# Tree attention: K and Q of heads 16 to 47 and 56 to 63 laid side by side by GpSimd before they are transposed

## The chip, the cores and the metric

The kernel runs on one core of one Trainium2 chip. The core has five engines with a queue of their own each: TensorE (PE, with its weight loads listed apart as PEld), VectorE (DVE), ScalarE (ACT), GpSimd (POOL) and SyncE (SP), and 16 DMA engines that they share. Each queue runs in order; queues wait for one another by semaphores. The metric is device time in microseconds (us) from launch to end, as the median of several executions.

## The reference

There are 96 heads (8 x 12) of 512 rows of 64 numbers in fp32. Row i is a node of a binary tree, and may look at itself and at its ancestors alone:

```python
mask = np.zeros((seq, seq))
for i in range(seq):
    mask[i, i] = 1
    parent = i
    while parent > 0:
        parent = (parent - 1) // 2
        mask[i, parent] = 1

scores = np.einsum('bhqd,bhkd->bhqk', Q, K) * scale
scores = scores + (1 - mask) * (-1e9)
weights = np.exp(scores - np.max(scores, axis=-1, keepdims=True))
weights = weights / (np.sum(weights, axis=-1, keepdims=True) + 1e-10)
return np.einsum('bhqk,bhkd->bhqd', weights, V).astype(np.float32)
```

## The kernel before

**Tiling.** Heads go in pairs: iteration i works on two heads, which stand in the upper and the lower 64 partitions of the scores' operands, and there are 48 pairs (NP). Pairs 0 to 7 (heads 0 to 15) have a layout of their own ("narrow"); from pair 8 on ("wide", WIDE = 8) K and Q come in with two heads side by side over the partitions. K and Q are loaded in blocks of 8 heads (KB), fp32 in HBM to bf16 in SBUF, into the tiles kst and qst, each with four buffers. V is loaded in blocks of 16 heads (VB = 16) into vst (three buffers), and its rows are then spread by DVE, ACT and POOL into the tiles vt (two sets), in the order that the tree needs (`spread`, L364).

**One iteration** has these steps, each named by a letter in the strings that set the order of PE's work (FIRST for i below 9, then "SVK" for odd i and "SVQ" for even i):

- S: the scores of pair i. Matmuls with mask codes (L511, L544) and with K and Q (L519, L554) go into PSUM, ACT takes the exponential (L529, L560).
- V: the values of pair i - 1. 20 small matmuls (L605) into ob; DVE takes the reciprocal of the sums (L651) and multiplies (L653) into the output tile of.
- K or Q: a turn. `wide_k` or `wide_q` transposes K or Q of two later pairs (four heads) through PE into ktp or qtp in PSUM, and DVE copies these into kq (L470, L474, L478 for K, L493 for Q). K of pairs 4b and 4b + 2 (block b) is turned in iterations 4b - 3 and 4b - 1, Q in 4b - 2 and 4b.
- DVE's and ACT's share of V's spreading.

**A turn** has eight slots. In blocks that are not in LAID each slot takes two transposes of 64 columns, one for each head, straight from kst or qst (`turn_slot`, L450). In blocks of LAID, which are 8 to 11 (heads 64 to 95), POOL has first laid the rows of two heads next to each other (`lay`, L433), in the one tile besideK or the one tile besideQ, with a half (g) for each turn; the turn then takes one transpose of 128 columns for a slot (L441). Since there is one such tile for each name, a half can be laid anew only when PE has turned what stood in it.

**The order on POOL** is a list written out by hand (`pool_program`): the loads, the stores, its share of the spreading, and the lays. An entry is put into the program at the first iteration in which `ready` allows it, and POOL runs them in that order. Each DMA issued by POOL takes the next of eight semaphores (DMASW0 to DMASW7) and waits until the DMA that had it eight places earlier has landed.

**The order within V**: the products are `firsts` (128 columns of e), `wholes` (128) and `halves` (64). Up to pair 27 `halves` come last, from pair 28 (4 * LAID[0] - 4) they stand between the other two.

Of the kernel before, what the change touches and what calls it, by code (L numbers as in the profile page):

```python
# [119 lines left out]
def kernel(  # L120
# [7 lines left out]
    nc = tc.nc  # L128
# [7 lines left out]
    WIDE = 8  # L136
    KB, VB, VO = 8, 16, 16
    EIGHT = 2
    LAID = (8, 9, 10, 11)
    assert NH % VB == 0  # L140

    fp32 = mybir.dt.float32
# [90 lines left out]
    issued = {(name, h) for name in ("kst", "qst") for h in (0, 1)}  # L233
# [35 lines left out]
    def head(i, a):  # L269

        return 2 * i + a if i < WIDE else 4 * (i // 2) + i % 2 + 2 * a
# [151 lines left out]
    def slots(st, i):  # L423
        return st[2 * i // KB].rearrange("p (g x) t d -> p g (x t) d", x=2)

    def lay(name, b):

        st = {"kst": ksts, "qst": qsts}[name][b]
        assert all((name, h) in issued for h in range(KB * b, KB * b + KB))
        laid[name, b] = two = beside[name[0].upper()]  # L430
        for g in range(KB // 4):
            src = st[:, 4 * g:4 * g + 4, :, :].rearrange("p (a x) t d -> p (x t) a d", x=2)
            nc.gpsimd.tensor_copy(  # L433
                out=two[:, g, :, :, :].bitcast(int32), in_=src.bitcast(int32)
            )

    def turn_slot(dst, name, i, s, out):

        two = laid.get((name, 2 * i // KB))
        if two is not None:  # L440
# [5 lines left out]
            return  # L446
        assert 2 * i // KB not in LAID
        st = slots({"kst": ksts, "qst": qsts}[name], i)
# [143 lines left out]
    def values(i):  # L592

        if i < NP - 1:
            obs[i] = ob = psO.tile([P, 2, 512], fp32, name="ob")
        else:
            obs[i] = ob = psS.tile([P, 2, 512], fp32, name="s1")
        e1, e2, vt = ets[i], e2s[i % NE], vts[(head(i, 0) // VB) % NV]

        vtile = VTILE if i < WIDE else WVTILE  # L600
        parts = EIGHT_PARTS if head(i, 0) >= VB * EIGHT else PARTS[i >= WIDE]
        assert all(("vt", n, head(i, a)) in issued for n in parts for a in range(2))

        def product(e, a, t, tile_v, lo=0, hi=128, **flags):
            nc.tensor.matmul(  # L605
                out=ob[lo:hi, a, 65 * t:65 * t + 65],
                lhsT=e[:, a, PLACE[t], lo:hi],
                rhs=vt[vtile[tile_v][0]][:, head(i, a) % VB, vtile[tile_v][1], 0:D + 1],
                **flags,
            )  # L610

        def firsts(a):
            for t in range(4):
                product(e1, a, t, 0, start=t == 0, stop=False)

        def halves(a, last=True):
            for t in (0, 1):
                product(e2, a, t, 1 + SELF[t], 0, 64, start=False, stop=last and t == 1)
                product(e2, a, t, 1 + t, 64, 128, start=False, stop=last and t == 1)

        def wholes(a, last=False):
            for t in (2, 3):
                product(e2, a, t, 1 + t, start=False, stop=last and t == 3)

        if i == NP - 1:
            for a in range(2):
                firsts(a)
                wholes(a)
                halves(a)
        elif i >= 4 * LAID[0] - 4:  # L630
            for a in range(2):
                firsts(a)
            for a in range(2):
                halves(a, False)
            for a in range(2):
                wholes(a, True)
        else:
            for a in range(2):
                firsts(a)
                wholes(a)  # L640
            for a in range(2):
                halves(a)
# [33 lines left out]
    def pool_program():  # L676

        ops = [
            (load_k, 2, 2), (load_q, 2, 2), (load_v, 0, 4), (load_v, 4, 4),
            (load_k, 4, 4), (load_q, 4, 4), (load_k, 8, 4),  # L680
            (load_q, 8, 4), (load_v, 8, 8), (load_k, 12, 4),
            (load_q, 12, 4), (load_k, 16, 8), (load_q, 16, 4), (load_rows, 1, "upper"),
            (load_rows, 1, "even"), (load_rows, 1, "odd"), (load_q, 20, 4),
            (load_k, 24, 8), (load_q, 24, 8), (load_rows, 2, "upper"),
            (load_k, 32, 8), (load_leaves, 2, 0), (load_leaves, 2, 1),
            (load_q, 32, 8), (load_rows, 3, "upper"),
            (spread_pool, (1, "Z0", 8, 16), (1, "Z1", 8, 16)),
            (load_k, 40, 8), (load_q, 40, 8), (load_leaves, 3, 0), (load_leaves, 3, 1),
            (spread_top, 2, 0, 16), (spread_pool, (2, "Z0", 0, 16), (2, "Z1", 0, 16)),
            (load_q, 48, 8), (spread_pool, (2, "X", 0, 16)),  # L690
            (load_k, 48, 8), (spread_pool, (2, "N", 0, 16)),
            (load_rows, 4, "upper"), (spread_top, 3, 0, 16),
            (load_k, 56, 8), (load_q, 56, 8), (load_leaves, 4, 0), (load_leaves, 4, 1),
            (spread_pool, (3, "X", 0, 16), (3, "N", 0, 16), (3, "Z0", 0, 16), (3, "Z1", 0, 16)),
            (load_k, 64, 8), (store_rows, 0, 2), (load_q, 64, 8), (store_rows, 2, 4),
            (load_k, 72, 8), (spread_top, 4), (store, nc.gpsimd, 4, 12), (lay, "kst", 8),
            (load_q, 72, 8), (spread_pool, (4, "X", 0, 16), (4, "N", 0, 16)),
            (lay, "qst", 8), (load_rows, 5, "upper"),
            (spread_pool, (4, "Z0", 0, 16), (4, "Z1", 0, 16)),
            (load_leaves, 5, 0), (load_leaves, 5, 1), (load_k, 80, 8), (load_q, 80, 8),  # L700
            (store, nc.gpsimd, 16, 8), (lay, "kst", 9), (load_k, 88, 8), (load_q, 88, 8),
            (lay, "qst", 9), (store, nc.gpsimd, 24, 8), (store, nc.gpsimd, 32, 16),
            (spread_top, 5), (lay, "kst", 10), (store, nc.gpsimd, 48, 16), (lay, "qst", 10),
            (spread_pool, (5, "X", 0, 16), (5, "N", 0, 16)),
            (spread_pool, (5, "Z0", 0, 16), (5, "Z1", 0, 16)),
            (lay, "kst", 11), (store, nc.gpsimd, 64, 8), (lay, "qst", 11),
            (store, nc.gpsimd, 72, 8), (spread_leaves, 5, 1),
            (store, nc.gpsimd, 80, 8), (store, nc.gpsimd, 88, 4),
        ]
        return ops  # L710
# [54 lines left out]
    def spread_by(copy, table, i):  # L765

        for args in table.get(i, []):
            spread(copy, *args)

    program = pool_program()  # L770

    def pool(i):
# [23 lines left out]
    for i in range(NP + 1):  # L796
        steps = FIRST[i] if i < len(FIRST) else "SVK" if i % 2 else "SVQ"
        for step in steps:
            if step == "S" and i < NP:
                scores1(i)  # L800
                scores2(i)
            if step == "V" and i >= 1:
                values(i - 1)
                norm(i - 1)
                valued = True
            if step == "K" and kdone < NP:
                kdone = turn("kst", kdone)
            if step == "Q" and qdone < NP:
                qdone = turn("qst", qdone)
            if step == "W":  # L810
                nc.scalar.copy(
                    out=codes[64:64 + CODE_ROWS, 1280:1536], in_=codes[0:CODE_ROWS, 1280:1536]
                )
            if step == "X":
                spin("s1" if valued else "ob", 2)
            if step == "D":
                spread_by(nc.vector.tensor_copy, BY_VECTOR, i)
            if step == "A":
                spread_by(nc.scalar.copy, BY_SCALAR, i)
        if "D" not in steps:  # L820
            spread_by(nc.vector.tensor_copy, BY_VECTOR, i)
        if "A" not in steps:
            spread_by(nc.scalar.copy, BY_SCALAR, i)
        pool(i)
# [32 lines left out]
```

## Time and profile before

| What | Value |
|---|---|
| Time, median of 3 runs | 133.55 us (133.35 to 133.63) |
| The profiled execution: its own time | 133.8 us |
| Its span, first to last instruction | 131.9 us |
| Mean granted TensorE clock | 0.978 |
| HBM read, written | 37.96 MB, 12.58 MB |
| Mean DMA rate | 245 GB/s |

The DMA rate counts bytes as they are moved into SBUF: loads turn fp32 into bf16, so that stages of pure loading show about 200 GB/s and stages of pure storing about 400. Busy time of an engine is the time covered by its instructions; issuing a DMA counts on POOL in these rows as a DMA_DIRECT2D instruction. In the timeline a row is: start, time covered, engine, line of the kernel, operation, what is written <- what is read, how many instructions are merged, and in brackets the idle time before it with what ended it. A row of stages is: the stage, its length, then busy time (and instructions) of the engines, the granted clock, the DMA share and GB/s.

### The profile page before, as it was taken

How to read it: one execution, taken by the hardware profiler on the slowest of the kernel's cores; microseconds unless marked ns; L12 is line 12 of the kernel's file. 1: busy time of each engine (PE TensorE's matmuls, PEld its weight loads, DVE VectorE, ACT ScalarE, POOL GpSimd, SP SyncE). 2: the span in 40 equal slices, each digit the busy share in tenths (PEclk: the TensorE clock that was granted, in tenths of full speed). 3: DMA queues.
4: the chain of work that ended last, by engine and by line, in shares of the span. 5: the costliest groups of instructions: out<-in, count | busy, mean ns of one | idle time of the engine just before them, and what ended most of it. 6: DMA issues, size and time to landing. Idle time of an engine off the chain costs nothing.

```text
span 131.9 us, 5281 instructions
## 1 busy us (share of the span) xinstructions
PE 114.7 (87%) x2286; PEld 80.4 (61%) x2289; DVE 108.8 (82%) x261; ACT 94.4 (72%) x153; POOL 87.1 (66%) x118
## 2 busy tenths in 40 slices
PE   6883999999789699899899999999988999999920
PEld 2351576676566476666577677677765766776610
DVE  3438569988999989989999999999999999877350
ACT  4358268989768957968858787787868668688900
POOL 6994624245623998799951899999999977802200
PEclk9999599999999999999999999999999999999996
DMA  3999999999999999999999999999999999999984
GB/s 122 216 190 196 198 199 205 199 199 207 206 200 205 204 202 208 209 202 205 202 208 204 244 236 305 338 204 207 203 288 285 228 391 406 400 402 402 397 315 148
DMA packets 29719, 32.28 MB, mean 245 GB/s; under 512 B 1488, under 2 KB 26704, under 8 KB 29696
## 3 DMA queue, kind: packets, MB, share of 16 engines
q0 software_dynamic: 28416, 30.68, 115.2%
q1 hardware_dynamic: 864, 0.93, 2.1%
q10 hardware_dynamic: 416, 0.33, 1.0%
q8 instruction: 18, 0.29, 0.8%
q14 instruction: 5, 0.04, 0.1%
HBM read 37.96 MB, written 12.58 MB: 383 GB/s over the span
## 4 chain that ended last, share of the span: by engine, by line
DVE 38%; PE 24%; DMA 14%; POOL 10%; issue 5%; ACT 3%; ACTq 1%; POOLq 0%
DVE of L653 12%; DVE vt L364 11%; DMA kst<-in_K_dram 8%; PE ob L605 8%; DMA qst<-in_Q_dram 6%; POOL vt L364 5%; DVE rec L651 3%; PE s L511 3%; DVE kq L493 3%; DVE kq L470 3%; DVE kq L478 3%; DVE kq L474 3%; PE s L519 2%; ACT e L560 2%; PE s L544 1%
## 5 line engine op out<-in xcount | busy, mean ns | idle before, releaser
L529 ACT ACTIVATE e<-s 128x1024 bf16<-128x1024 f32 x40 | 40.9, 1023 | 20.7 <-PE s L519 20.1
L605 PE MATMUL ob<-vt,e 128*128 128x65 bf16 (+1 forms) x940 | 39.8, 198 | 6.0 <-DVE of L653 3.0
L605 PEld LDWEIGHTS <-e 128*128 128x128 bf16 (+1 forms) x960 | 31.7, 103 | 15.9 <-DVE of L653 5.1
L560 ACT ACTIVATE e<-s 128x384 bf16<-128x384 f32 x80 | 34.7, 491 | 0.0
L653 DVE TENSOR_TENSOR of<-ob,rec 128x512 f32<-128x512 f32 x47 | 32.5, 691 | 1.6
L364 POOL COPY vt<-vst 32x512 int32<-32x512 int32 (+1 forms) x38 | 31.0, 816 | 2.9 <-PE ob L605 1.2
L364 DVE COPY vt<-vst 32x1024 bf16<-32x1024 bf16 (+6 forms) x54 | 26.8, 497 | 2.3 <-DMA vst<-in_V_dram 1.3
L662 POOL DMA_DIRECT2D out_dram<-of x13 | 12.1, 928 | 12.7 <-DVE of L653 9.2
L511 PE MATMUL s<-codes 40*128 40x512 bf16 x96 | 19.3, 398 | 0.7 <-ACT e L525 0.4
L519 PE MATMUL s<-kq 64*128 64x512 bf16 x96 | 18.5, 380 | 0.0
L651 DVE RECIPROCAL rec<-ob 128x8 f32<-128x8 f32 x47 | 9.6, 204 | 8.8 <-PE ob L605 8.0
L554 PEld LDWEIGHTS <-kq 64*128 64x128 bf16 x320 | 12.1, 94 | 4.8
L554 PE MATMUL s<-kq 64*128 64x160 bf16 (+1 forms) x320 | 14.6, 208 | 0.0
L544 PE MATMUL s<-codes 40*128 40x384 bf16 x80 | 13.6, 333 | 0.3
L493 DVE COPY kq<-qtp 128x1024 bf16<-128x1024 bf16 x20 | 13.6, 681 | 0.0
L256 POOL DMA_DIRECT2D qst<-in_Q_dram x11 | 8.3, 752 | 6.8 <-DMA vst<-in_V_dram 2.6
L525 ACT ACTIVATE e<-s 128x1024 bf16<-128x1024 f32 x8 | 8.2, 1022 | 6.0 <-PE s L519 5.9
L544 PEld LDWEIGHTS <-codes 40*128 40x128 bf16 x80 | 6.1, 94 | 7.9 <-issue 1.2
L256 POOL DMA_DIRECT2D kst<-in_K_dram x10 | 7.6, 760 | 3.9 <-PE ob L605 2.8
L470 DVE COPY kq<-ktp 128x256 bf16<-128x256 bf16 x20 | 8.3, 415 | 0.3 <-PE ktp L450 0.3
L474 DVE COPY kq<-ktp 128x256 bf16<-128x256 bf16 x20 | 8.3, 415 | 0.0
L478 DVE COPY kq<-ktp 128x512 bf16<-128x512 bf16 x20 | 8.3, 414 | 0.0
(49 smaller groups left out, 139.4 us busy)
## 6 DMA issues: line engine op xcount, KB each, us to landing
kst<-in_K_dram POOLq DMA_DIRECT2D x10, 512.0 KB, 13.2
out_dram<-of POOLq DMA_DIRECT2D x5, 1024.0 KB, 13.9
qst<-in_Q_dram POOLq DMA_DIRECT2D x9, 512.0 KB, 14.5
out_dram<-of POOLq DMA_DIRECT2D x2, 2048.0 KB, 20.8
vst<-in_V_dram POOLq DMA_DIRECT2D x12, 256.0 KB, 14.9
vst<-in_V_dram POOLq DMA_DIRECT2D x6, 512.0 KB, 14.3
out_dram<-of POOLq DMA_DIRECT2D x1, 1536.0 KB, 10.7
qst<-in_Q_dram POOLq DMA_DIRECT2D x5, 256.0 KB, 11.9
```

The lines of the kernel that those rows point to most:

```text
L256: return nc.gpsimd.dma_start(out=kept[b][:, h0 % KB:h0 % KB + n, :, :].rearrange("p (g x) t d -> p g (x t d)", x=2), in_=wide[:, h0 // 2:( ...
L364: return copy(out=dst, in_=src)
L493: nc.vector.tensor_copy(out=qq[:, :, 0:16, :].rearrange("p b u c -> p b (u c)"), in_=halves)
L511: nc.tensor.matmul(out=sp[:, a, :], lhsT=(k1code if i < WIDE else k1wide)[64 * a:64 * a + CODE_ROWS, :], rhs=(q1code[64 * a:64 * a + CODE_ ...
L519: nc.tensor.matmul(out=sp[:, a, :], lhsT=keys(i, a, TOP), rhs=qTs[i][64 * a:64 * a + 64, :, :].rearrange("p t c -> p (t c)"), start=False, ...
L529: ) if i < WIDE else nc.scalar.activation(
L544: nc.tensor.matmul(out=flat[:, a, :, :].rearrange("p u (t c) -> p u t c", t=4)[:, :, :, 16:64], lhsT=k2wide[64 * a:64 * a + CODE_ROWS, :], ...
L554: nc.tensor.matmul(out=flat[:, a, :, lo:hi], lhsT=keys(i, a, WTILE2[t]), rhs=qT[64 * a:64 * a + 64, :, lo:hi], start=False, stop=t == 1, s ...
L560: nc.scalar.activation(out=e2s[i % NE][:, a, :, 32:128].rearrange("p t (r u) -> p t r u", u=2), in_=flat[:, a, :, :].rearrange("p u (t r) ...
L605: nc.tensor.matmul(out=ob[lo:hi, a, 65 * t:65 * t + 65], lhsT=e[:, a, PLACE[t], lo:hi], rhs=vt[vtile[tile_v][0]][:, head(i, a) % VB, vtile ...
L651: nc.vector.reciprocal(out=rec[:, a:a + n, :, :], in_=o4[:, a:a + n, :, D:D + 1])
L653: nc.vector.tensor_tensor(out=ofs[g][:, first:last + 1:step, :, :], in0=o4[:, a:a + n, :, 0:D], in1=rec[:, a:a + n, :, :].to_broadcast([P, ...
```

## The change

Blocks 2, 3, 4, 5 and 7 (heads 16 to 47 and 56 to 63) join LAID. `lay` can lay one half alone. The point from which V takes its other order stays at pair 28, now as LATE. In POOL's list the lays of these blocks are added, the spreading of the top rows of V's block 3 (`spread_top`, 3) moves behind the loads of block 7 and the leaves of V's block 4, and the third and fourth of four small stores are issued one at a time.

```diff
-    LAID = (8, 9, 10, 11)
+    LAID = (2, 3, 4, 5, 7, 8, 9, 10, 11)
+    LATE = 28
...
-    def lay(name, b):
+    def lay(name, b, g0=0, g1=2):
...
-        for g in range(KB // 4):
+        for g in range(g0, g1):
...
-        elif i >= 4 * LAID[0] - 4:
+        elif i >= LATE:
...
-            (load_k, 24, 8), (load_q, 24, 8), (load_rows, 2, "upper"),
-            (load_k, 32, 8), (load_leaves, 2, 0), (load_leaves, 2, 1),
-            (load_q, 32, 8), (load_rows, 3, "upper"),
-            (spread_pool, (1, "Z0", 8, 16), (1, "Z1", 8, 16)),
-            (load_k, 40, 8), (load_q, 40, 8), (load_leaves, 3, 0), (load_leaves, 3, 1),
+            (load_k, 24, 8), (load_q, 24, 8), (load_rows, 2, "upper"), (lay, "kst", 2),
+            (load_k, 32, 8), (lay, "qst", 2, 0, 1), (load_leaves, 2, 0), (load_leaves, 2, 1),
+            (load_q, 32, 8), (lay, "qst", 2, 1, 2), (load_rows, 3, "upper"),
+            (spread_pool, (1, "Z0", 8, 16), (1, "Z1", 8, 16)), (lay, "kst", 3),
+            (load_k, 40, 8), (load_q, 40, 8), (lay, "qst", 3),
+            (load_leaves, 3, 0), (load_leaves, 3, 1), (lay, "kst", 4),
             (spread_top, 2, 0, 16), (spread_pool, (2, "Z0", 0, 16), (2, "Z1", 0, 16)),
-            (load_q, 48, 8), (spread_pool, (2, "X", 0, 16)),
+            (load_q, 48, 8), (lay, "qst", 4), (spread_pool, (2, "X", 0, 16)),
             (load_k, 48, 8), (spread_pool, (2, "N", 0, 16)),
-            (load_rows, 4, "upper"), (spread_top, 3, 0, 16),
-            (load_k, 56, 8), (load_q, 56, 8), (load_leaves, 4, 0), (load_leaves, 4, 1),
+            (load_rows, 4, "upper"), (lay, "kst", 5),
+            (load_k, 56, 8), (load_q, 56, 8), (lay, "qst", 5),
+            (load_leaves, 4, 0), (load_leaves, 4, 1), (spread_top, 3, 0, 16),
             (spread_pool, (3, "X", 0, 16), (3, "N", 0, 16), (3, "Z0", 0, 16), (3, "Z1", 0, 16)),
-            (load_k, 64, 8), (store_rows, 0, 2), (load_q, 64, 8), (store_rows, 2, 4),
-            (load_k, 72, 8), (spread_top, 4), (store, nc.gpsimd, 4, 12), (lay, "kst", 8),
+            (load_k, 64, 8), (store_rows, 0, 2), (load_q, 64, 8), (store_rows, 2, 3),
+            (lay, "kst", 7), (store_rows, 3, 4),
+            (load_k, 72, 8), (lay, "qst", 7), (spread_top, 4), (store, nc.gpsimd, 4, 12), (lay, "kst", 8),
```

How this stands in the queues, at three places. The line numbers of the changed kernel are one higher than before in these functions; x2 is two instructions alike.

On POOL, where block 4 (heads 32 to 39) is about to be turned; the rows start with the two loads of V's leaves of block 3. Before:

```order
L294 DMA vst<-in_V_dram 32x8x512 x2
L364 COPY vt_0_107<-vst 32x16x32 x4
L364 COPY vt_1_108<-vst 32x32x32 x2
L256 DMA qst<-in_Q_dram 128x4x512
L364 COPY vt_2_109<-vst 32x32x32
```

and now:

```order
L295 DMA vst<-in_V_dram 32x8x512 x2
L434 COPY besideK<-kst 128x512 x2
L365 COPY vt_0_107<-vst 32x16x32 x4
L365 COPY vt_1_108<-vst 32x32x32 x2
L257 DMA qst<-in_Q_dram 128x4x512
L434 COPY besideQ<-qst 128x512 x2
L365 COPY vt_2_109<-vst 32x32x32
```

K of block 4 has come in between the DMA issues and six V copies, Q of block 4 behind these and behind another load.

On PE, the first turn of Q of block 4, with the last product of V ahead of it. Before:

```order
L605 LDWEIGHTS e_1_103
L605 MATMUL ob<-vt_1_114,e_1_103 64x65
L450 LDWEIGHTS qst [waits DMASW7_49]
L450 MATMUL qtp<-ptile,qst 64x2x64
L450 LDWEIGHTS qst
```

and now:

```order
L606 LDWEIGHTS e_1_103
L606 MATMUL ob<-vt_1_114,e_1_103 64x65
L442 LDWEIGHTS besideQ [waits Pool_49]
L442 MATMUL qtp<-ptile,besideQ 128x2x64
L442 LDWEIGHTS besideQ
```

The turn waited for a load that had landed, and now waits for POOL's copy; of 16 pairs of instructions eight are left.

On POOL, the lay of K of block 8 (heads 64 to 71), with a store ahead of it and the load of Q of block 9 behind. Before:

```order
L662 DMA out_dram<-of 128x12x256 [waits DMASW3_49]
L433 COPY besideK<-kst 128x512 [waits DMAHW1_49,DMASW4_49,Pool_49]
L433 COPY besideK<-kst 128x512
L256 DMA qst<-in_Q_dram 128x4x512
L364 COPY vt_2_109<-vst 32x32x32 [waits PE_49,Pool_49]
```

and now:

```order
L663 DMA out_dram<-of 128x12x256 [waits DMASW3_49]
L434 COPY besideK<-kst 128x512 [waits DMASW4_49,PE_49,Pool_49]
L434 COPY besideK<-kst 128x512 [waits PE_49]
L257 DMA qst<-in_Q_dram 128x4x512
L365 COPY vt_2_109<-vst 32x32x32 [waits Pool_49]
```

Both halves now wait for PE, the second for the second turn of block 7, which stood in it.

More of the change, by code (lines that the diff above doesn't have):

```diff
@@ L424, in slots @@
         return st[2 * i // KB].rearrange("p (g x) t d -> p g (x t) d", x=2)
-    def lay(name, b):
+    def lay(name, b, g0=0, g1=2):
         st = {"kst": ksts, "qst": qsts}[name][b]
-        assert all((name, h) in issued for h in range(KB * b, KB * b + KB))
+        assert all((name, h) in issued for h in range(KB * b + 4 * g0, KB * b + 4 * g1))
         laid[name, b] = two = beside[name[0].upper()]
-        for g in range(KB // 4):
+        for g in range(g0, g1):
             src = st[:, 4 * g:4 * g + 4, :, :].rearrange("p (a x) t d -> p (x t) a d", x=2)
```

## The prediction

> **What bounds the kernel now.** I read the busy rows and the slices of the page first, then busy time by stage, then the timeline of the engines that wait on one another in heads 16 to 63. The page:
>
> ```profile
> span 131.9 us, 5281 instructions
> PE 114.7 (87%) x2286; PEld 80.4 (61%) x2289; DVE 108.8 (82%) x261; ACT 94.4 (72%) x153; POOL 87.1 (66%) x118
> DVE  3438569988999989989999999999999999877350
> POOL 6994624245623998799951899999999977802200
> DMA  3999999999999999999999999999999999999984
> ```
>
> Two resources are full almost throughout: the DMA engines from the second slice on, and VectorE (DVE) from a fifth of the span on. GpSimd (POOL) has gaps in the first half and none from slice 24 to 32. By stage (columns: stage, length, then busy PE, PEld, DVE, ACT, POOL, clock, DMA share, GB/s):
>
> ```profile
> 40.00:48.00 8.00, 6.63 (x154) 4.74 (x153) 7.40 (x17) 5.76 (x10) 5.76 (x9) 1.00 1.30 203
> 48.00:56.00 8.00, 7.36 (x175) 5.35 (x172) 7.78 (x19) 6.53 (x11) 6.58 (x9) 1.00 1.25 206
> 56.00:64.00 8.00, 7.56 (x179) 5.48 (x180) 7.37 (x18) 5.98 (x11) 7.82 (x10) 1.00 1.31 204
> 64.00:72.00 8.00, 7.43 (x175) 5.32 (x170) 7.71 (x19) 5.89 (x10) 4.37 (x6) 1.00 1.25 206
> 88.00:96.00 8.00, 7.84 (x150) 5.81 (x146) 7.75 (x18) 6.38 (x12) 7.91 (x11) 1.00 1.30 204
> ```
>
> Between 40 and 72 us DVE is idle for 0.60, 0.22, 0.63 and 0.29 us of each 8, 1.74 in all: work that comes late on DVE there is not made up again. At the end the last store cannot start before DVE's last product, and the DMA engines are full until shortly before it (slices of 0.3 us from 120 us on):
>
> ```profile
> DMA  9999899999999999998999996434999973100000
> GB/s 410 410 423 451 341 382 382 396 382 423 437 369 396 382 423 410 382 410 341 410 369 423 437 369 273 137 137 164 396 369 372 382 249 119 41 10 0 0 0 0
> ```
>
> Only the four slices at 127.2 to 128.4 lie open; at 400 GB/s their 273, 137, 137 and 164 are 1.2 - 0.3 x 711/400 = 0.67 us lost. The bytes stay the same, so compute that ends earlier can win about 0.7 us; compute that ends later costs all of it.
>
> **The change part by part.** It takes 160 transposes and their weight loads from PE (five blocks x two names x 16), gives POOL 20 copies, and makes PE's turns wait for these. What a turn costs in either form is in the profile, since heads 64 to 95 are laid already. The first four rows are one unlaid iteration (values, turn, scores, values), the others a laid one:
>
> ```profile
> 58.07 0.79 PE L605 MATMUL ob<-vt,e 128*128 128x65 bf16 x20
> 58.69 0.61 PE L450 MATMUL qtp<-ptile,qst 128*64 128x128 bf16 x16
> 59.23 0.40 PE L511 MATMUL s<-codes 40*128 40x512 bf16 x2
> 60.18 0.79 PE L605 MATMUL ob<-vt,e 128*128 128x65 bf16 x20
> ...
> 85.24 0.89 PE L605 MATMUL ob<-vt,e 128*128 128x65 bf16 x20
> 85.97 0.61 PE L441 MATMUL qtp<-ptile,besideQ 128*128 128x128 bf16 x8
> 86.51 0.40 PE L511 MATMUL s<-codes 40*128 40x512 bf16 x2
> 87.43 0.89 PE L605 MATMUL ob<-vt,e 128*128 128x65 bf16 x20
> ```
>
> *Removed.* From the turn's start to the next scores' start is 59.23 - 58.69 = 0.54 us with 16 transposes and 86.51 - 85.97 = 0.54 with eight. Two transposes of 64 columns run side by side and take the time of one of 128. Half the instructions, no time: 0. The DVE copies out of ktp and qtp are the same, 0.
>
> *The width of the turn.* Up to iteration 28 the values end in products of 64 columns, and only from there on (LATE) in products of 128. A turn of 128 columns behind 64-wide products is a sequence that before never runs. The nearest rows: values to turn is 58.69 - 58.07 = 0.62 us where the widths change once less, 85.97 - 85.24 = 0.73 where the 64-wide products stand in the middle. So one more change of width costs 0 to 0.11 us, on 20 turns 0 to 2.2 us of PE. PE sits idle for 0.64 us of the 8 from 48 to 56 and mostly waits for DVE; I take 0.3, since the lower end is hidden work and only a part of the iterations follows PE. The Trainium skill, page TensorEngine Tiling (Array Packing), Key Properties, says that a change of tiling mode drains TensorE; by it the price would be paid at each of the 20 turns, and the sum would be 1.9 us higher if nothing hid it. The 0.11 us agrees in sign.
>
> *Added on POOL.* One block's K copies and Q copies, and what stands around the first wait that I expect:
>
> ```profile
> 42.41 0.58 POOL L294 DMA_DIRECT2D vst<-in_V_dram  x1 [1.92 <-DMA kst<-in_K_dram]
> 43.03 4.86 POOL L364 COPY vt<-vst 32x512 int32<-32x512 int32 x6
> 47.84 0.76 POOL L256 DMA_DIRECT2D qst<-in_Q_dram  x1
> 46.91 0.61 PE L450 MATMUL ktp<-ptile,kst 128*64 128x128 bf16 x16
> 49.01 0.61 PE L450 MATMUL qtp<-ptile,qst 128*64 128x128 bf16 x16
> ...
> 77.44 1.20 POOL L433 COPY besideK<-kst 128x512 int32<-128x512 int32 x2
> 79.26 0.61 PE L450 MATMUL ktp<-ptile,kst 128*64 128x128 bf16 x16
> 92.17 1.39 POOL L433 COPY besideQ<-qst 128x512 int32<-128x512 int32 x2
> 94.97 0.61 PE L441 MATMUL qtp<-ptile,besideQ 128*128 128x128 bf16 x8
> ```
>
> K costs 1.20 us and Q 1.39, a block 2.59, five blocks 12.95 us on POOL, all between 24 and 77 us. POOL has room for it in sum; the question is where in its queue it stands.
>
> *The wait at block 4.* The leaves' DMA ahead starts at 42.41, when a transfer has landed that the change does not move, and ends at 42.99. Then, in the new order: K of block 4 (1.20) to 44.19, the same six V copies (4.86) to 49.05, the load of Q (0.76) to 49.81, the first half of Q of block 4 (1.39/2 = 0.70) to 50.51. PE wants to turn that half at 49.01. PE waits 50.51 - 49.01 = 1.50 us. Behind it on PE stand the scores of the next iteration; ACT's exponentials wait for these, and DVE for its copy of the turn and for the next values. Bounds: 0.9 where compute comes 0.6 late to this point already (below), 1.5 where it is on time. I take 1.4 and no further lateness ahead of it in that sum.
>
> *The other places.* Up to block 3 each copy stands behind a DMA issue that waits for the same landing, so the data are there; the first half of Q of block 3 is done at 37.63 + 0.74 + 0.70 = 39.07 against a turn at 39.02, which is 0.05 us and dropped:
>
> ```profile
> 37.63 0.74 POOL L256 DMA_DIRECT2D qst<-in_Q_dram  x1 [1.99 <-PE ktp L450]
> 39.02 0.61 PE L450 MATMUL qtp<-ptile,qst 128*64 128x128 bf16 x16
> ```
>
> For blocks 5 and 7 the same addition along POOL's queue, with PE 1.4 us late, has the first halves done over 1 us before their turns. K of block 8 is new in one point: its second half overwrites what the turn at 79.26 reads, so it starts at 79.26 + 0.61 = 79.87 and not at 78.04 (77.44 + half of 1.20). From there to 93.56 POOL has hardly a gap, so all of it comes 1.83 us late: Q of block 9, whose first half was laid at 92.17 + 0.70 = 92.87, now at 94.70, against a turn at 94.97. That leaves 0.27 us, whatever the lateness of compute, which shifts both. Taken as 0, bounds 0 to 1.8.
>
> *POOL against DVE.* DVE's own V copies (32 partitions x 512 elements) take longer when POOL copies at the same time. The first row ran beside a DMA issue, the other two beside POOL copies; then all of DVE's V copies in a stage without POOL copies and in one full of them:
>
> ```profile
> 63.41 0.42 DVE L364 COPY vt<-vst 32x1024 bf16<-32x1024 bf16 x1
> 48.97 0.98 DVE L364 COPY vt<-vst 32x1024 bf16<-32x1024 bf16 x1
> 60.65 0.79 DVE L364 COPY vt<-vst 32x1024 bf16<-32x1024 bf16 x1
> ...
> 64.00:72.00 8.00, 1.67 (x4) 1.00 1.25 206
> 96.00:104.00 8.00, 2.42 (x3) 1.00 1.17 273
> ```
>
> 0.42 us each against 0.81. The new 12.95 us cover a quarter of the 52 us from 24 to 76, in which DVE makes about 28 such copies: 7 more meet a POOL copy, at 0.39 us at most 2.7 us, at half of it (a meeting is not always whole) 1.4. DVE's idle time takes up a part; I count 0.6, bounds 0 and 2.7. The Trainium skill, page SBUF — State Buffer, section "Who interferes with whom", holds that a VectorE copy in a two-port mode and a GpSimd instruction exclude one another for a whole instruction, while PE and ACT never wait. By it every meeting may cost up to the rest of a POOL copy, 0.6 to 0.7 us here, and 7 meetings would make 4 to 5 us instead of 0.6 (a rival, below). The trace shows 0 to 0.56 a meeting, less than that.
>
> *DMA.* The order of the transfers is the same. POOL issues those from 50 to 70 us up to 4 us later (12.95 us of copies less its gaps). The page shows the DMA engines full and this long from issue to landing, so the queue does not run dry: 0. Buffers come free earlier, but the issues wait for the transfer eight places back in the order, not for buffers: 0.
>
> ```profile
> kst<-in_K_dram POOLq DMA_DIRECT2D x10, 512.0 KB, 13.2
> ```
>
> Sum: 1.4 + 0.3 + 0.6 + 0 = 2.3 us. The profiled execution took 133.8 us (span 131.9 and 1.9 around it) and would take 136.1; the median of the three runs is 133.55, 0.25 lower, so I predict **135.9 us**.
>
> **The rivals.** *POOL becomes the bound behind K of block 8.* The 0.27 us at Q of block 9 is used up by slower POOL copies; then POOL, not DVE, paces heads 64 to 95. Its stage is 7.91 of 8 busy. From the point where POOL loses more than 0.27 us between 79.9 and 93.6 each further loss is paid; at 10% longer copies and issues 1.4 us, less 0.27, on top of 2.3: 137.0. *Full exclusion.* Each of the 7 new meetings holds DVE for a whole POOL copy of 0.70 us: 4.9, less the 1.74 us in which DVE is idle, is 3.2 in place of 0.6: 138.5. For it speaks the 0.98 row, against it the 0.42 to 0.81 of the others; the Trainium skill's page on SBUF, cited above, would have it so. *The wait is hidden.* If PE, ACT and DVE hold enough work queued at 49 us, the late turn costs nothing, as the scores that need it come two iterations later; against it, PE is in order and DVE idles at once. Then only a collision or two remain: 133.6. *Faster.* If 160 fewer weight loads and transposes let PE hand over earlier in the unlaid stage, compute ends earlier, up to the 0.7 us that the DMA engines leave: 132.9. The equal 0.54 us speaks against it, and so does DVE's load.
>
> **How the numbers follow.** Forecast, slower by the wait and the collisions (134.2 to 137.5): 0.60. POOL bound (136.5 to 139): 0.11. Full exclusion (138 to 139): 0.05. Hidden, within 0.3 us: 0.11. Faster: 0.13. Range 133.3 to 138.0: it leaves out most of the faster case, the upper third of the POOL case and full exclusion, 0.19 together. A change of 0.2%, 0.27 us, is about the least that a measurement of this kernel tells from none. Faster by more 0.13, same 0.11, slower 0.76.
>
> **What would show it.** PE busy within 2 us of 114.7 with 160 fewer matmuls, a turn still 0.54 us from start to scores; POOL about 100 us busy; POOL as releaser of PE's weight loads (besideQ) near 49 us, about 1.5 us long, and nowhere else above 0.3; DVE's V copies longer by 1 to 2 us in sum; the second K copy of block 8 waiting for PE; DMA still full to within 2 us of the last store. I am wrong if no PE wait stands there, if turns get shorter than 0.54 us, or if DMA slices before 120 us fall below full.

## The result, and the profile after

| | Before | Changed |
|---|---|---|
| Median | 133.52 us (6 runs, 133.08 to 133.63) | 137.76 us (6 runs, 137.05 to 138.11) |
| Ratio | 1 | 1.0315, interval 1.0281 to 1.0350 |
| Measured again, other runs of before beside it | 133.64 us | 137.41 us (6 runs), 1.0287 (1.0258 to 1.0315) |

The changed kernel is 3.8 to 4.2 us slower. The time lies inside the predicted range, but 1.5 to 1.9 us above the predicted 135.9. A few executions of some kernels are slower than the rest (169 us against 134 at the most): medians are of all executions, the ratios leave those few out. The profiled execution took 138.11 us. Its page:

```profile
span 136.3 us, 4978 instructions
PE 115.3 (85%) x2126; PEld 81.3 (60%) x2129; DVE 110.3 (81%) x261; ACT 94.4 (69%) x153; POOL 99.7 (73%) x138
DVE  3436469988999985989999999999999999777340
DMA  4999999999999999999999999989999999999993
...
L365 DVE COPY vt<-vst 32x1024 bf16<-32x1024 bf16 (+6 forms) x54 | 28.0, 519 | 3.4 <-DMA vst<-in_V_dram 2.4
```

PE has 160 matmuls fewer and is as busy as before (114.7); POOL has its 20 copies more. Two marks are new. DVE has a 5 in its sixteenth slice (51.1 to 54.5 us) where before has a 9, and DMA has an 8 that before does not have (88.6 to 92.0 us). Both are waits.

**The first wait** is at Q of block 4. Two stages of the changed kernel (columns as in the prediction):

```profile
40.00:48.00 8.00, 7.05 (x138) 5.10 (x136) 7.76 (x19) 6.96 (x13) 4.52 (x8) 1.00 1.31 203
48.00:56.00 8.00, 6.69 (x132) 4.86 (x128) 6.11 (x16) 4.46 (x8) 7.77 (x10) 1.00 1.25 206
```

Its timeline, first PE's and then POOL's:

```profile
49.84 0.78 PE L606 MATMUL ob<-vt,e 128*128 128x65 bf16 x20
51.93 0.62 PE L442 MATMUL qtp<-ptile,besideQ 128*128 128x128 bf16 x8 [1.31 <-POOL besideQ L434]
...
43.90 0.58 POOL L295 DMA_DIRECT2D vst<-in_V_dram  x1 [2.58 <-DMA kst<-in_K_dram]
44.47 1.17 POOL L434 COPY besideK<-kst 128x512 int32<-128x512 int32 x2
45.70 4.80 POOL L365 COPY vt<-vst 32x512 int32<-32x512 int32 x6
50.46 0.76 POOL L257 DMA_DIRECT2D qst<-in_Q_dram  x1
51.26 1.16 POOL L434 COPY besideQ<-qst 128x512 int32<-128x512 int32 x2
```

POOL does what the prediction laid out, in that order. PE stands for 1.31 us, and DVE, whose stage from 48 to 56 us was 7.78 us busy before, falls to 6.11. Compared with before, this turn comes 2.92 us later (51.93 against 49.01): 1.31 us are this wait, and PE was 1.61 us late already when it began. Not all of that is owed to the change: at the turn at 22.13 us (21.12 before), ahead of the first new copy at 25.60, this execution is 1.0 us late. PE's list of waits shows that POOL's lays hold PE up nowhere else in this execution:

```profile
PE ob L606 <- DVE of L654: 3.8, 10, 0.9
...
PE qtp L442 <- POOL besideQ L434: 1.3, 1, 1.3
```

**The second wait** is POOL's own, at K of block 8. POOL's timeline in the changed kernel:

```profile
79.39 1.05 POOL L663 DMA_DIRECT2D out_dram<-of  x1
80.49 0.61 POOL L434 COPY besideK<-kst 128x512 int32<-128x512 int32 x1
83.82 0.61 POOL L434 COPY besideK<-kst 128x512 int32<-128x512 int32 x1 [2.71 <-PE ktp L442]
84.37 0.76 POOL L257 DMA_DIRECT2D qst<-in_Q_dram  x1
...
83.13 0.62 PE L442 MATMUL ktp<-ptile,besideK 128*128 128x128 bf16 x8
```

The last row is the turn of block 7 on PE that the second copy waits for; before it stands at 79.26. In the kernel before, the same store and the same load (Q of block 9) are these:

```profile
76.34 1.05 POOL L662 DMA_DIRECT2D out_dram<-of  x1
78.59 0.76 POOL L256 DMA_DIRECT2D qst<-in_Q_dram  x1
```

The store comes 3.05 us later than before and the load 5.78: POOL waits for a turn that is itself 3.87 us late. What the DMA engines make of that is seen in the DMA view from 84 to 94 us, in slices of 0.25 us, for the changed kernel:

```profile
DMA  9999665453999999899999433395979999999999
GB/s 373 426 373 356 242 262 213 164 229 119 258 205 217 225 180 209 131 193 188 225 201 221 74 61 49 29 53 72 104 96 168 203 199 199 197 199 201 201 197 193
```

Each digit below 9 is a slice in which the engines were partly idle. Most of them stand at 85.0 to 86.5 us, ahead of the late load, and from 89.5 on, ahead of the next one (V's rows, issued at 88.80 and at 83.00 before). Counting (10 - digit) tenths of 0.25 us for each, 1.7 us of DMA time are lost here; in the kernel before every digit of this view is a 9. Coarse as these digits are, the same count serves for all the kernels below.

### The profile page after: what moved, and what is told of

It reads as the page before. It is cut to its first block, busy times and chain, and to the rows that moved or that the text cites. A ratio compares the mean times of both kernels' runs of the same rounds, so it can differ in the third digit from the quotient of the medians.

```text
span 136.3 us, 4978 instructions
## 1 busy us (share of the span) xinstructions
PE 115.3 (85%) x2126; PEld 81.3 (60%) x2129; DVE 110.3 (81%) x261; ACT 94.4 (69%) x153; POOL 99.7 (73%) x138
## 4 chain that ended last, share of the span: by engine, by line
DVE 37%; DMA 25%; PE 17%; POOL 7%; issue 7%; ACT 1%; ACTq 1%; POOLq 0%
DMA vst<-in_V_dram 17%; DVE of L654 12%; DVE vt L365 9%; DMA qst<-in_Q_dram 9%; PE ob L606 7%; DVE kq L494 4%; DVE rec L652 4%; POOL vt L365 3%; DVE kq L475 3%; DVE kq L479 3%; DVE kq L471 3%; PE s L512 2%; PE qtp L442 2%; PE s L520 2%; PE ktp L442 1%
## 5 line engine op out<-in xcount | busy, mean ns | idle before, releaser
L365 DVE COPY vt<-vst 32x1024 bf16<-32x1024 bf16 (+6 forms) x54 | 28.0, 519 | 3.4 <-DMA vst<-in_V_dram 2.4
L434 POOL COPY besideK<-kst 128x512 int32<-128x512 int32 x18 | 11.2, 647 | 3.1 <-PE ktp L442 2.7
L442 PE MATMUL qtp<-ptile,besideQ 128*128 128x128 bf16 x144 | 11.1, 219 | 1.3 <-POOL besideQ L434 1.3
L442 PE MATMUL ktp<-ptile,besideK 128*128 128x128 bf16 x144 | 11.1, 219 | 0.3 <-DVE kq L479 0.3
L434 POOL COPY besideQ<-qst 128x512 int32<-128x512 int32 x18 | 11.2, 651 | 0.1
```

Source lines behind the costliest of these rows:

```text
L365: return copy(out=dst, in_=src)
L434: nc.gpsimd.tensor_copy(out=two[:, g, :, :, :].bitcast(int32), in_=src.bitcast(int32))
L442: nc.tensor.transpose(out=out(dst), in_=two[:, 2 * i % KB // 4, s, :, :].rearrange("p a d -> p (a d)"), identity=ptile[:, 0:128],)
```

## The experiments

**The changed kernel once more**, for a second trace beside the experiments.

> The changed kernel itself, beside the next three on one chip. Both theories: the ratio of its first measurement, 1.028 to 1.035; the profile shows PE waiting for POOL at Q of block 4 for 1.2 to 1.5 us again.

1.0287. PE waits three times for POOL's lays here, at Q of blocks 2, 3 and 4:

```profile
27.66 0.62 PE L442 MATMUL qtp<-ptile,besideQ 128*128 128x128 bf16 x8 [0.86 <-POOL besideQ L434]
39.06 0.62 PE L442 MATMUL qtp<-ptile,besideQ 128*128 128x128 bf16 x8 [0.35 <-POOL besideQ L434]
50.60 0.62 PE L442 MATMUL qtp<-ptile,besideQ 128*128 128x128 bf16 x8 [1.97 <-POOL besideQ L434]
```

The last wait is longer than expected, because PE is ready earlier (at 48.63, before at 49.01). The first half of Q of block 4 is laid at 50.52 (49.94 and half of 1.16), where the prediction had worked out 50.51. POOL's stop at K of block 8 is 3.47 us, and the count of lost DMA time from 84 to 94 us is 2.1 us. The turn of block 7 there starts at 82.38 us, 3.1 later than before. Its last store in the list of DMA issues (the last number is the time from issue to landing):

```profile
out_dram<-of SPq DMA_DIRECT2D x1, 512.0 KB, 4.5
```

and of the kernel before:

```profile
out_dram<-of SPq DMA_DIRECT2D x1, 512.0 KB, 3.6
```

By the timelines these stores are issued at 130.61 and at 127.41 us. So the last landing is 4.1 us later: 3.2 are late compute, and 0.9 is a longer queue of stores in front of the last one. Of these 3.2 us, 3.1 were lost by the turn at 82.38 already.

**Q of block 4 laid earlier.**

```diff
-            (load_leaves, 3, 0), (load_leaves, 3, 1), (lay, "kst", 4),
+            (load_leaves, 3, 0), (load_leaves, 3, 1), (lay, "kst", 4), (lay, "qst", 4),
...
-            (load_q, 48, 8), (lay, "qst", 4), (spread_pool, (2, "X", 0, 16)),
+            (load_q, 48, 8), (spread_pool, (2, "X", 0, 16)),
```

> The changed kernel, with the lay of Q of block 4 moved up in POOL's list, directly behind the lay of K of block 4 and ahead of the six V copies. Theory (PE's wait of 1.31 us on this copy is passed on whole): the wait is gone, the time is 1.2 to 1.5 us below the changed kernel's 137.8, so 136.3 to 136.6 (ratio to before 1.020 to 1.023). Rival (the wait only uncovers DVE's collisions or the drained DMA queue behind it): the time stays within 0.4 us of 137.8 (ratio 1.029 to 1.034).

140.2 us, 1.0487 (1.0452 to 1.0523), slower still. The test misfired: the data had not landed at the earlier place. Its timeline, POOL's first and then PE's:

```profile
47.81 1.17 POOL L434 COPY besideQ<-qst 128x512 int32<-128x512 int32 x2 [3.78 <-DMA qst<-in_Q_dram]
...
57.66 0.96 PE L606 MATMUL ob<-vt,e 128*128 128x65 bf16 x16 [2.04 <-POOL vt L365]
59.10 1.03 PE L442 MATMUL ktp<-ptile,besideK 128*128 128x128 bf16 x8 [0.48 <-POOL besideK L434]
```

and two of its stages:

```profile
56.00:60.00 4.00, 1.86 (x24) 1.50 (x23) 1.12 (x3) 0.24 (x1) 3.91 (x6) 0.58 1.16 181
60.00:64.00 4.00, 4.00 (x48) 2.65 (x48) 2.73 (x7) 1.79 (x3) 3.96 (x7) 0.57 1.27 184
```

POOL stands for 3.78 us until Q has landed, its V copies come late, PE waits 2.04 us for one of them, and then the granted clock is 0.58 and 0.57 for 8 us, in which a turn's eight transposes cover 1.03 us and not 0.62. Since every queue is in order, a lay that waits for data costs what stands behind it. This run can't price the wait at block 4, so a later run leaves the lay out.

**The laid turns of blocks 2 to 7 done as two transposes of 64 columns each**, from the same tiles, so that the values and the turn have the widths of before.

```diff
+        if two is not None and 2 * i // KB < 8:
+            for a in range(2):
+                nc.tensor.transpose(
+                    out=out(dst[64 * a:64 * a + 64]),
+                    in_=two[:, 2 * i % KB // 4, s, a, :],
+                    identity=ptile[:, 0:128],
+                )
+            return
```

> The changed kernel, but blocks 2, 3, 4, 5 and 7 are turned by two transposes of 64 columns for a slot again, out of the laid copies: all waits on POOL are as in the changed kernel, only the width of the turn is as before. Theory (one more change of width on PE costs 0.11 us on each of 20 turns): values to scores 1.16 us as before and not 1.27, and the time is 0.5 to 2.2 us below 137.8 (ratio 1.015 to 1.028). Rival (DVE paces these iterations, so PE's 0.11 is hidden): the turn gets shorter and the time stays within 0.4 us of 137.8 (ratio 1.029 to 1.034).

137.36 us, 1.0301 (1.0260 to 1.0342): no difference from the changed kernel that can be told. Values, turn and scores of one iteration in the changed kernel's timeline:

```profile
39.88 0.79 PE L606 MATMUL ob<-vt,e 128*128 128x65 bf16 x20
40.60 0.62 PE L442 MATMUL qtp<-ptile,besideQ 128*128 128x128 bf16 x8
41.15 0.40 PE L512 MATMUL s<-codes 40*128 40x512 bf16 x2
```

and in that of this kernel:

```profile
38.30 0.79 PE L614 MATMUL ob<-vt,e 128*128 128x65 bf16 x20
38.92 0.61 PE L443 MATMUL qtp<-ptile,besideQ 128*64 128x128 bf16 x16
39.47 0.40 PE L520 MATMUL s<-codes 40*128 40x512 bf16 x2
```

From values to scores it is 41.15 - 39.88 = 1.27 us with turns of 128 columns and 39.47 - 38.30 = 1.17 with turns of 64. The 0.10 us of the change of width are there. Twenty of them, 2 us, are not in the time; a few tenths of a microsecond the interval can't exclude. The turn itself takes 0.55 us in both.

**The copies made and not used.** POOL lays all blocks as in the changed kernel, but PE turns blocks 2 to 7 straight from kst and qst.

```diff
-        two = laid.get((name, 2 * i // KB))
+        two = laid.get((name, 2 * i // KB)) if 2 * i // KB >= 8 else None
```

> POOL's list is the changed kernel's, with all 20 new copies, but PE turns blocks 2, 3, 4, 5 and 7 from kst and qst as before, so that nothing waits for the new copies. It measures POOL's extra 13 us alone. Theory (waits and width of PE make most of the loss, collisions with DVE 0.6 us, at most 2.7): 134.0 to 135.2 (ratio 1.004 to 1.013). Rival (the collisions on DVE and late DMA issues make most of it): 136 or more (ratio above 1.018).

134.73 us, 1.0088 (1.0055 to 1.0121). A second run of the same kernel gives its profile.

> The run whose copies nothing waits for, once more, for a profile without a drop of TensorE's clock in mid-span. Theory (collisions of POOL's copies with DVE's own): ratio 1.005 to 1.012, DVE's V copies 1 to 2 us longer in sum than before's. Rival (the rest comes from late DMA issues): DVE's V copies as before's within 0.5 us, and DMA slices below full in mid-span.

135.01 us (10 runs), 1.0078 (1.0043 to 1.0112), the profiled one at 135.18. From its page:

```profile
PE 113.0 (85%) x2289; PEld 79.3 (59%) x2289; DVE 112.1 (84%) x261; ACT 94.4 (71%) x153; POOL 99.3 (74%) x138
DMA  4999999999999999999999999999999999999964
...
L365 DVE COPY vt<-vst 32x1024 bf16<-32x1024 bf16 (+6 forms) x54 | 30.0, 555 | 2.7 <-DMA vst<-in_V_dram 1.8
```

The DMA engines stay full, so that no DMA time is lost to late issues; no turn of blocks 2 to 7 waits for a lay, and K of block 8 need not wait for one. What is left is 3.2 us more in DVE's 54 V copies (30.0 against 26.8; 1 to 2 were expected), and 1.0 to 1.2 us of time. PE's list of waits suggests a way from the one to the other: its waits for DVE's products and for DVE's V copies sum to 5.7 and 3.2 us, where before has 3.0 and 1.2. So 1.0 to 1.2 us is what POOL's extra copies cost when nothing waits for them. That they cost it by way of DVE is argued and not shown: PE also waits 0.53 us for POOL itself (at 75.43), and the last run below has waits for DVE's products almost as long without being slower.

**No block laid at all**, from the kernel before: LAID empty, the lays of blocks 8 to 11 left out too, and V's order as in the first pairs throughout.

> The kernel before with no lays at all: blocks 8 to 11 too are turned by two transposes of 64 columns for a slot, and V keeps its first order to the end. POOL loses 16 copies (10 us) between 77 and 111 us. Theory (laying buys PE no time and costs collisions on DVE and a change of width on PE): faster than before by 0.3 to 1.0 us, not more since the DMA engines are full (ratio 0.992 to 0.998). Rival (laying wins something that the timeline of the turn does not show): slower than before, ratio above 1.004.

134.91 us, 1.0079 (1.0050 to 1.0108). DVE's V copies fall to 26.0 us, and still the kernel is slower. PE's timeline behind 60 us shows six stops with no releaser, 3.3 us in all; the kernel before has none there. The three longest:

```profile
99.95 0.47 PE L451 MATMUL qtp<-ptile,qst 128*64 128x128 bf16 x10 [0.62 <-issue]
...
112.49 0.33 PE L451 MATMUL ktp<-ptile,kst 128*64 128x128 bf16 x5 [1.13 <-issue]
...
118.96 0.50 PE L606 MATMUL ob<-vt,e 128*128 128x65 bf16 x11 [0.63 <-issue]
```

These sum to 2.4 us. "issue" is time in which PE waited for nothing that the profile shows; why it stood stays open.

**Q of block 4 not laid**, its turn straight from qst.

```diff
-            (load_q, 48, 8), (lay, "qst", 4), (spread_pool, (2, "X", 0, 16)),
+            (load_q, 48, 8), (spread_pool, (2, "X", 0, 16)),
```

> The changed kernel, but Q of block 4 alone is turned from qst as before and not laid. Theory (PE's wait at Q of block 4 is passed on whole, and POOL has 1.2 us less to do behind it): 1.2 to 1.8 us below the changed kernel (ratio 1.018 to 1.024). Rival (DVE's collisions and the stretch behind 76 us decide, the wait is taken up there): within 0.4 us of the changed kernel (ratio 1.028 to 1.035).

136.61 us, 1.0210 (1.0181 to 1.0240), 0.77% or 1.0 us below the changed kernel's second measurement. The last store is issued at 128.61, 2.0 us earlier than in the changed kernel's second trace, and takes 4.2 us in place of 4.5. So compute wins 2.0 us in this execution and its span 2.3, more than the medians differ: its time of 136.63 us has 2.8 us outside its span, where that of the second trace has 1.8. POOL still stops for 2.72 us at K of block 8, and the count of lost DMA time from 84 to 94 us is 0.57 us.

**The second half of K of block 8 laid later**, behind a load and two V copies, when its turn has come by.

```diff
-            (load_k, 72, 8), (lay, "qst", 7), (spread_top, 4), (store, nc.gpsimd, 4, 12), (lay, "kst", 8),
-            (load_q, 72, 8), (spread_pool, (4, "X", 0, 16), (4, "N", 0, 16)),
+            (load_k, 72, 8), (lay, "qst", 7), (spread_top, 4), (store, nc.gpsimd, 4, 12), (lay, "kst", 8, 0, 1),
+            (load_q, 72, 8), (spread_pool, (4, "X", 0, 16), (4, "N", 0, 16)), (lay, "kst", 8, 1, 2),
```

> The changed kernel, but the second half of K of block 8 is laid behind the load of Q of block 9 and four V copies, so that POOL does not stand for 2.7 us until PE has turned the end of block 7. Theory (nothing waits for what POOL does there, the DMA queue that ran dry has no one waiting for it): within 0.4 us of the changed kernel (ratio 1.028 to 1.035), with DMA full at 84 to 92 us. Rival (the stop makes POOL and the DMA engines late, and that is 0.5 to 1.5 us of the loss): ratio 1.020 to 1.028.

136.0 us, 1.0184 (1.0157 to 1.0212), 1.03% or 1.4 us below the changed kernel's second measurement. The load of Q of block 9 is issued at 79.29, and POOL's next stop, 1.41 us at Q of block 8, comes behind it. Its DMA view from 84 to 94 us (0.33 us lost by the count), and the last store in the list of DMA issues:

```profile
DMA  7999999999969888999999999999999999999999
...
out_dram<-of SPq DMA_DIRECT2D x1, 512.0 KB, 2.8
```

The last store is issued at 130.27 us, 0.34 earlier than in the changed kernel's second trace, and then takes 2.8 us in place of 4.5. So most of the gain is in the queue, not in compute.

**Both edits.**

> Both of the last two edits in the changed kernel. Theory (what is left is the collisions, 1.1 us by the run whose copies nothing waits for, and a little for PE's width): 1.2 to 1.8 us below the changed kernel, ratio 1.016 to 1.024. Rival (POOL's stop counts as well and the two add): ratio 1.008 to 1.016.

134.98 us (12 runs), 1.0077 (1.0046 to 1.0107). Apart the edits win 0.77% and 1.03%, together 2.10%, more than the 1.80% of their sum but within the intervals. What remains, 0.77% or 1.0 us, is as much as the unused copies cost. No DMA time is lost from 84 to 94 us. (Its profiled execution, at 133.56 us, is 1.4 below the median; nothing more is read from it.)

**The transfers first, and K of block 8 as one.** This tells the two readings of that stop apart. If POOL's copies of heads 64 to 95 came too late for PE, a lay that goes on waiting in front of them must go on costing; if the DMA queue ran dry, it is enough to give the queue its two next loads ahead of the lay.

```diff
-            (load_k, 72, 8), (lay, "qst", 7), (spread_top, 4), (store, nc.gpsimd, 4, 12), (lay, "kst", 8),
-            (load_q, 72, 8), (spread_pool, (4, "X", 0, 16), (4, "N", 0, 16)),
-            (lay, "qst", 8), (load_rows, 5, "upper"),
+            (load_k, 72, 8), (lay, "qst", 7), (spread_top, 4), (store, nc.gpsimd, 4, 12), (load_q, 72, 8),
+            (load_rows, 5, "upper"), (lay, "kst", 8), (spread_pool, (4, "X", 0, 16), (4, "N", 0, 16)),
+            (lay, "qst", 8),
```

> The changed kernel, with two DMA issues (the load of Q of block 9, 512 KB, and the upper rows of V's block 5, 512 KB) moved ahead of the lay of K of block 8. POOL still stands there until PE has turned the end of block 7, and its copies come as late as in the changed kernel; only the DMA queue gets 1 MB more before the stop. Theory (the stop costs through the DMA queue that runs dry and is paid when the last stores queue up): 0.7 to 1.6 us below the changed kernel's 137.4 to 137.8 (ratio 1.017 to 1.024), DMA fuller at 84 to 92 us, and the last stores land sooner. Rival (the stop costs through POOL's late copies, which PE and DVE wait for): within 0.4 us of the changed kernel (ratio 1.026 to 1.035).

136.38 us, 1.0188 (1.0142 to 1.0235), the same as with the lay in halves. POOL's timeline:

```profile
82.37 0.61 POOL L434 COPY besideK<-kst 128x512 int32<-128x512 int32 x1 [1.18 <-PE ktp L442]
83.04 2.22 POOL L365 COPY vt<-vst 32x1024 int32<-32x1024 int32 x2
```

Its DMA view from 84 to 94 us (0.10 us lost), and the last store:

```profile
DMA  9989999999999999999999999999998999999999
...
out_dram<-of SPq DMA_DIRECT2D x1, 512.0 KB, 2.8
```

POOL still stops (1.18 us), and its V copies start at 83.04, where the lay in halves has them at 80.09. Three microseconds of lateness on POOL's V copies cost nothing that the times show; a full DMA queue wins all that the lay in halves won. The last store is issued at 130.29 us, 0.02 from the other.

**Only blocks 10 and 11 laid**, from the kernel before, with V's other order from pair 36, as a try for a version better than both: the stops of the kernel with no block laid stand from 99.95 us on, where the last blocks are turned, so the lays of blocks 8 and 9 might be spared.

> The kernel before with lays for blocks 10 and 11 alone (V's second order from pair 36). Without any lays PE stood three times for 2.4 us in all with no releaser in the profile, all of them at turns or values behind 99 us, when stores fill the DMA engines. Theory (fewer instructions on PE matter there alone, and lays of blocks 8 and 9 cost collisions): 0.2 to 0.7 us faster than before (ratio 0.994 to 0.999). Rival (what was tuned together belongs together: POOL's stores come earlier and loads later): ratio 1.000 to 1.008.

133.75 us (12 runs), 1.0004 (0.9986 to 1.0023): the same as before. The lays of blocks 10 and 11 with that order win back the 0.8% that the kernel without any lost, and PE's timeline has no stop without a releaser behind 60 us; those of 8 and 9 neither win nor cost. No version here beats the kernel before. One more thing can be read from this run. First PE's waits for DVE's products in the run with unused copies, then the same here:

```profile
PE ob L605 <- DVE of L653: 5.7, 13, 1.4
...
PE ob L606 <- DVE of L654: 5.4, 14, 0.9
```

DVE's V copies sum to 27.7 us here, 0.9 more than before, although POOL is less busy (82.6 us against 87.1). Neither sum tells by itself that a kernel is slower.

## Why the prediction was right in its sign and short in its size

The runs take the 3.8 us of the changed kernel's second measurement apart. By the intervals of the ratios each measured term holds to about 0.5 us:

| Term | Predicted, us | Measured, us | By |
|---|---|---|---|
| PE waits at Q of block 4 | 1.4 | 1.0 | lay left out: 1.0287 to 1.0210 |
| K of block 8: POOL stops, DMA runs dry | 0 | 1.4 | lay in halves: 1.0287 to 1.0184; loads first: 1.0188 |
| POOL's copies beside DVE's | 0.6 | 1.0 to 1.2 | copies unused: 1.0078 and 1.0088 |
| Width of the turn | 0.3 | none told, 2 us excluded | turns of 64 columns: 1.0301 |
| Sum | 2.3 | 3.4 to 3.6 | of 3.8; the rest is within the intervals, and the first two together give 2.8 |

- **The wait at Q of block 4** was right: its place, its releaser, and what is queued behind it. 1.50 us were worked out from POOL's queue, 0.9 if compute came late; 1.31 and 1.97 stand in the two traces, and 1.0 is what its removal wins. Smaller waits at Q of blocks 2 and 3 (0.86 and 0.35 us in the second trace, none in the first) were put at 0; PE's next turn of K, at 46.38 us, is no later than before (46.91).
- **The failed step is "so the queue does not run dry: 0".** The prediction compared one lateness, POOL's from 50 to 70 us, with the 13.2 us from issue to landing and went no further along the queue. It had the other in hand, that the second half of K of block 8 must wait for PE's turn, 1.83 us behind its old place. But it priced that stop against PE's turn at 94.97 alone, where a late compute shifts both sides, and not for the loads that stand behind the stop, where it adds. In the first trace the turn is 3.87 us late; with the 1.83 that makes 5.7 of the 5.78 us by which the load of block 9's Q is late. The 13.2 us were no measure of the reserve either: that is a median over K's loads, while a store was the last transfer ahead of this gap, and stores move at 356 to 426 GB/s in the first slices of the DMA view above, twice the pace of loads. The first gap comes at 85.0 us, 5.6 us behind the start of that store's issue (79.39) and not 13.2.
- **Where that loss is paid** is the end. Compute goes on: in the second trace it is 3.1 us late at the turn at 82.38 and 3.2 at the last store. But later transfers move back, and the last store lands 4.5 us after its issue, where the two kernels with the gap nearly closed have 2.8. The prediction had named this as what would show it wrong (DMA slices below full before 120 us), and it came.
- **The rival "POOL becomes the bound behind K of block 8"** gave 137.0, near the time, for a wrong reason. Behind block 4 PE waits for no lay in either trace, and with the loads first POOL's late copies cost nothing. A number that fits is no proof of its mechanism. That the time lies inside the range at all is in part luck: the upper end of 138.0 was there for this rival, and it covered a loss by another path.
- **The collisions** were in the bounds (0 to 2.7 us) and taken too low. DVE's V copies grew by 1.2 and 1.8 us in the two traces of the changed kernel (1 to 2 were foretold) and by 3.2 with unused copies, so that this sum varies with how the copies fall. The time does not follow it: with blocks 10 and 11 alone laid the sum grew by 0.9 us, and the time is that of before. So the price of the unused copies is measured, and its way through DVE stays open. Full exclusion would have had 3.2 us of time, and falls. By the rule of the Trainium skill, page SBUF — State Buffer, section "Who interferes with whom", a whole POOL copy could be lost at each meeting; the trace agrees with the sign and shows less: 3.2 us for 20 copies of about 0.65 us, 0.16 us for each POOL copy.
- **The width** was right as a price (0.10 us a turn against at most 0.11). Its term of 0.3 us is too small for these times to tell from none. By the Trainium skill, page TensorEngine Tiling (Array Packing), Key Properties, a change of tiling mode drains TensorE; at 0.10 us a turn, 20 turns would add 2 us if nothing hid them, which the equal times of both widths exclude.
- **Removed work at no gain** was right: 160 transposes less, and a turn of 0.55 us as before. "Faster" falls with it. "Hidden" falls with PE's 1.31 us and DVE's stage from 48 to 56 us.

## What to carry to other kernels

A queue that issues transfers and does other work too has a reserve: the bytes in flight behind the last issue, at the rate at which those very bytes drain. Add up all that makes an issue late, the lateness of the engine that the queue waits for included, and compare the sum with that reserve, before any single lateness is called free. Here such a stop was mended by putting the next transfers in front of it.

## What the runs showed of the hardware

- PE's clock fell behind a short wait in one execution. In the second trace of the changed kernel the wait at block 4 is 1.97 us, behind a stretch in which PE was busy for 0.64 us of 2, and the granted clock then is 0.51 and 0.63 for 4 us. In four other traces with this wait (the first trace, two transposes of 64 columns, K of block 8 in halves, loads first: 1.30 to 1.41 us) it stays at 1.00. Stages of the second trace:

```profile
48.00:50.00 2.00, 0.64 (x20) 0.47 (x17) 1.97 (x5) 1.44 (x3) 1.92 (x4) 1.00 1.27 205
50.00:52.00 2.00, 1.40 (x22) 0.95 (x22) 1.01 (x3) 0.12 (x1) 1.94 (x3) 1.00 1.24 208
52.00:54.00 2.00, 2.00 (x36) 1.75 (x28) 1.11 (x3) 1.66 (x3) 1.96 (x4) 0.51 1.24 205
54.00:56.00 2.00, 2.00 (x27) 1.01 (x25) 1.96 (x5) 0.68 (x1) 1.96 (x4) 0.63 1.25 207
```

- The Trainium skill, page TensorE: Matmul & The Clock Gate, section "What's actually happening", says that the clock falls to half after an idle window of about 3.4 us that runs freely. The half agrees (0.51 here, 0.57 with Q laid earlier); that one execution falls and another of the same kernel does not fits a window that runs freely, which no run here tests.
- PE's stops without a releaser in the kernel with no block laid (3.3 us in six places, all behind 87 us) may be what makes it slower, though its DVE copies are shorter. Their cause was not found.
